# Six of eight accumulators held in PSUM, two copied out by ScalarE, and angle tables built without GpSimd

## The chip, the core and the metric

The kernel runs on one core of a Trainium2 chip, as one program in one launch. The metric is the device time of an execution in microseconds. A core has five engines with one in-order queue of instructions each: TensorE (PE in the profile; its weight loads are PEld), VectorE (DVE), ScalarE (ACT), GpSimd (POOL) and SyncE (SP, which only starts transfers here). Matrix products go into PSUM, which has eight banks of 128 x 512 float32; the rest of the data is in SBUF.

## The reference

A two-layer streaming encoder on T = 576 tokens (a prompt of 512 and a sample of 64), width 1024. A layer is

- one input projection `h = x @ w_in`, split among three mixers: a diagonal state-space model (SSM), banded attention and a retention; each mixer's output is projected, multiplied by a sigmoid gate, and the three are summed, projected by `w_o` and normalised;
- PEER: 8 heads choose 16 experts each out of 128 x 128, and each chosen expert contributes

```
u = u_tab[expert]; act = gelu(u . x); out += gate * act * v_tab[expert]
```

- a gated per-layer input and a last normalisation.

The SSM state is `h_t = a h_(t-1) + b u_t` with complex `a`. The kernel runs it as a real scan after turning the input by `exp(-i theta t)` and turns the result back, so that it needs cos(theta t) and sin(theta t) for 8 blocks of 128 states a layer: two tables of 128 x 576 a block.

## The kernel before

All activations lie feature by token: `XH`, `XL` are eight blocks of 128 features x 576 tokens, the high and the low part of x in the format of the fast float32 product. A product is three matmuls (high x high, high x low, low x high). Weights come by SP into three buffers `wr` (512 KB a block); `split` (L203) makes `wh` with a ScalarE cast (L204) and `wl` with a subtraction (L205), four buffers each.

**Order.** The instructions of each engine are put in order by a planner when the program is made: it takes the program's order as priority and issues what is ready in its own simulated time. On the chip an engine then waits at its next instruction, whatever is behind it. In the first part of a layer, streams of steps (SSM, retention, projections, filling) are woven by `weave` (L137) on a rough clock for TensorE and VectorE.

**Tables.** `rotation` (L419) makes one block's two tables on GpSimd from `rot` (16 angles) and `rot16` (36 multiples of 16 angles): six instructions of 128 x 576. `rot16` is itself made by VectorE at the start, by doubling (L373 to L379). Layer 0 calls `rotation` in `begin` (L708), which is in the SSM stream. The tables of layer 1 are made during layer 0 by `next_tables` (L919), a step at every second step of the attention, and stored to DRAM by SP (L922); layer 1 loads them.

**Gates.** `filling` (L801) computes gate projections while the SSM and the retention hold TensorE up: the first GB = 8 of them, then it waits for the retention.

**Experts.** Tokens NG = 160 to 575 are done densely. `hidden(i)` (L1009) is the first product of the 128 experts with first key i: 24 matmuls of 416 columns into a `lin` bank, then gelu on ScalarE into `act`. The second product adds `v[i]` times gate times `act` to eight output blocks R[0..7]. Gates are built by one-hot products (L1210, L1211), copied by ScalarE (`gs`), stored to DRAM (`gd`), and read back as `gblk`. While the one-hots run, `prefetch` (L1017) computes `hidden` for N_EARLY = 34 experts, whose `act` go to DRAM, and for the first LA + GE = 8; by FR0 and FR its 42 x 8 steps are all placed before or among the one-hot products.

**The loop** (L1283) takes GE = 2 experts at a time. It computes `hidden` for the two that are LA = 6 ahead (or loads an early `act`), multiplies `act` by the gate (GpSimd for every fourth expert, VectorE for the others, L1302), splits it into `Wh`, `Wl`, and then for d = 0..7 does six matmuls (L1324). For d < HELD = 2 the sum stays in PSUM over the whole loop (one bank `bgd`, one `lin`); the other six go to one of four `aux` banks and VectorE adds each to R[d] (L1329). That leaves two `lin` banks to `hidden`. The other 160 tokens are done sparsely by VectorE in the same loop (`advance`, L1270): GpSimd gathers rows of u and v by index (L1237), VectorE takes dot products (L1243) and sums (L1255).

Of the kernel before, what the change touches and what calls it, by code (L numbers as in the profile page):

```python
# [46 lines left out]

GE = 2
LA = 6
N_EARLY = 34  # L50

GB = 8
GS = 7

UR = 0.7
# [10 lines left out]
LS = 0.5  # L66
LE = 0

GG = 4

HELD = 2

VR = 8
LEAD = 3
# [81 lines left out]
def body(ctx, tc, nc, A, O, depth=DEPTH, dbg=None):  # L156
# [153 lines left out]
    cre = cst.tile([128, nst], F32, name="cre")  # L310
    cim = cst.tile([128, nst], F32, name="cim")
    rot = [cst.tile([128, nst, 16], F32, name=f"rot{i}") for i in range(2)]
    rot16 = [cst.tile([128, nst, 36], F32, name=f"rq{i}") for i in range(2)]
    with ExitStack() as c0:
        p0 = pool(c0, "p0")
        t_ = lambda n: p0.tile([128, nst], F32, name=n)
# [53 lines left out]

        for m in (1, 2, 4, 8):
            double(V, rot[0], rot[1], 0, m)
        for i in range(2):  # L373
            V.memset(rot16[i][:, :, 0:1], 1.0 - i)
            V.tensor_copy(rot16[i][:, :, 1:2], rot[i][:, :, 15:16])
        for m in (1, 2, 4, 8, 16):
            double(V, rot16[0], rot16[1], 1, m)
        for i in range(2):
            V.tensor_copy(rot16[i][:, :, 32:36], rot16[i][:, :, 0:4])  # L379

    tables = dr.tile([8, 2, 128, T], F32, name="tables")
    for L in range(depth):
# [6 lines left out]
def run(steps, n=None):  # L389
    for _ in steps if n is None else zip(range(n), steps):  # L390
        pass
# [7 lines left out]
def mixers(tc, env):  # L399
# [6 lines left out]
    with ExitStack() as c:  # L406
# [1 line left out]
        rp = pool(ret, "rp")  # L408
        gt = pool(ret, "gt")
        M = []  # L410
        o36 = lambda t: t.rearrange("p (a b) -> p a b", b=16)

        def col(blk):
            clock[0] += 48 * HF / 2400
# [1 line left out]

        gates = {}

        def rotation(qq, pl, bufs):  # L419

            new = lambda n, b=1: pl.tile([128, T], F32, name=n, bufs=b)
            ct, sn, tx = new("ct", bufs), new("sn", bufs), new("tx")
            c1 = [e.rot16[i][:, qq, :, None].to_broadcast([128, 36, 16]) for i in range(2)]
            c2 = [e.rot[i][:, qq, None, :].to_broadcast([128, 36, 16]) for i in range(2)]
            G.tensor_mul(o36(ct), c1[0], c2[0])
            G.tensor_mul(o36(tx), c1[1], c2[1])
            G.tensor_sub(ct, ct, tx)
            tx = new("tx")
            G.tensor_mul(o36(sn), c1[0], c2[1])
            G.tensor_mul(o36(tx), c1[1], c2[0])  # L430
            G.tensor_add(sn, sn, tx)
            return ct, sn

        def col_steps(blk, out):
# [254 lines left out]
        def ssm():  # L689
# [18 lines left out]
            def begin(q):  # L708
                if L:
                    ct, st = wk("ct", 2), wk("sn", 2)  # L710
                    SY.dma_start(ct, e.tables[q, 0])
                    SY.dma_start(st, e.tables[q, 1])
                else:
                    ct, st = rotation(q, sp, 2)
                if q % 2 == 0:
                    yield from project(q)
                inputs[q] = ct, st, bus.pop(q)
# [111 lines left out]
        with ExitStack() as ca:  # L829
# [88 lines left out]

            def next_tables():  # L919
                for q in range(8):  # L920
                    for i, t in enumerate(rotation(L * 8 + 8 + q, pa, 1)):
                        SY.dma_start(e.tables[q, i], t)  # L922
                    yield

# [69 lines left out]
def peer_ple(tc, env):  # L994
# [8 lines left out]
    with ExitStack() as c:  # L1003
# [5 lines left out]
        def hidden(i):  # L1009
            w = weights(A["uT"][L, i], eng=by[0])  # L1010
            p = lin()
            yield from e.mm3_steps(p, w, XH, XL, (NG, T))
            act = ap_.tile([128, ND_T], F32, name="act", bufs=LA + GE)
            S.activation(act, p[:, :ND_T], AF.Gelu_apprx_tanh)
            acts[i] = act
# [265 lines left out]
        av = A["v"].rearrange("(a p) d -> a p d", p=128)  # L1281

        for e1 in range(0, 128 + LA, GE):  # L1283
            for i in range(e1, min(e1 + GE, 128)):
                if i in acts:
                    continue
                if i in early:
                    acts[i] = ap_.tile([128, ND_T], F32, name="act", bufs=LA + GE)
                    SY.dma_start(acts[i], ad[i])
                else:  # L1290
                    run(hidden(i))
            e0 = e1 - LA
            if e0 < 0:
                continue
            wv = []
            for i in range(e0, e0 + GE):
                act = acts.pop(i)
                if i % IB == 0:
                    gblk = lp.tile([128, NTG, IB, TG], F32, name="gblk", bufs=2)
                    SY.dma_start(gblk, gd[:, :, i:i + IB].rearrange("g j i t -> j g i t"))  # L1300
                a3 = act.rearrange("p (g t) -> p g t", t=TG)
                (G if GG and i % GG == 0 else V).tensor_mul(a3, a3, gblk[:, :, i % IB])  # L1302
                wh = lp.tile([128, ND_T], F32R, name="Wh", bufs=2 * GE)

                wl = (lp.tile([128, ND_T], F32R, name="Wl", bufs=2 * GE) if i > e0 else
                      vraw().bitcast(F32R)[:, :ND_T])
                split(wh, wl, act)
                wv.append(weights(av[L * 128 + i]) + (wh, wl))
# [4 lines left out]
                SY.dma_start(gb3[:, 0], A["ln3_g"][L])  # L1313
                SY.dma_start(gb3[:, 1], A["ln3_b"][L])
            if e0 == 0:
                held = [e.bgd(), lin()][:HELD]
            for a, b in ((NG, HF), (HF, T)) if fin else ((NG, T),):
                for d in range(ND):
                    hold = d < HELD
                    p = held[d][:, a - NG:b - NG] if hold else bank()[:, :b - a]  # L1320
                    w = slice(d * 128, (d + 1) * 128)
# [4 lines left out]
                                      stop=(j == GE - 1 and g == 2 and (fin or not hold)), skip_group_check=hold)  # L1326
                    if hold and not fin:
                        continue
                    V.tensor_add(R[d][:, a:b], R[d][:, a:b], p)  # L1329
            done = advance(done, (e0 + GE) / PACE)  # L1330
        m32 = load(lp, A["c_m32"], [128, NG2], "m32")
# [132 lines left out]
```

## Time and profile before

| | |
|---|---|
| median of 3 executions | 4293.08 us (4280.81 to 4308.05) |
| the profiled execution | 4261.82 us, span 4260.0 us |
| mean granted TensorE clock | 0.974 of full speed |
| busy: PE, PEld | 4050.0 us (95%), 3789.8 us (89%) |
| busy: DVE, ACT, POOL | 3433.5 us (81%), 1562.5 us (37%), 1435.8 us (34%) |

Times inside a profile count from the span's start. A row of the windows view is one stretch with the busy time and the number of instructions of each engine, the granted clock, and the share of time in which the 16 DMA engines were busy. A row of the waits view says which engine and line waited for which, for how long in total, how often, and the longest. In a timeline or a group of lines, `out<-in` are the program's names.

### The profile page before, as it was taken

The numbers are of one execution on the slowest core, as the hardware profiler recorded it, in microseconds if no ns is written. First come the engines' busy times: TensorE is split into PE (matmuls) and PEld (weight loads), VectorE is DVE, ScalarE is ACT, GpSimd is POOL, SyncE is SP. The second block draws the span as 40 slices with busy tenths as digits, with TensorE's granted clock in tenths as the row PEclk, the third lists the DMA queues.
The fourth block names the chain that finished last, engine by engine and source line by source line (L and its number), as shares of the span: only waits on it lengthen the run. The fifth ranks groups of instructions, "written<-read, shape, count | busy, mean of one in ns | idle before, by whom it ended". The sixth has DMA issues, their size and how long they took to land.

```text
span 4260.0 us, 65840 instructions
## 1 busy us (share of the span) xinstructions
PE 4050.0 (95%) x25032; PEld 3789.8 (89%) x25032; DVE 3433.5 (81%) x6827; ACT 1562.5 (37%) x2600; POOL 1435.8 (34%) x1050
## 2 busy tenths in 40 slices
PE   6998999898999999999999999999989999999998
PEld 6787899798999999999787889897989999999997
DVE  8944459987999989999678344698979999999985
ACT  3223433376333333333432243333843333233324
POOL 4634123301545445443100011332035444454421
PEclk8999999999999999999999999999999999999999
DMA  3123222277998989898232222124789999889961
GB/s 114 56 76 113 67 72 79 96 262 266 321 336 315 330 297 331 302 336 283 68 99 83 83 85 78 60 81 137 282 287 331 322 327 317 311 310 321 320 210 43
DMA packets 353886, 873.78 MB, mean 205 GB/s; under 512 B 33184, under 2 KB 169504, under 8 KB 350240
## 3 DMA queue, kind: packets, MB, share of 16 engines
q1 hardware_dynamic: 261408, 533.98, 36.4%
q0 software_dynamic: 92160, 335.59, 22.1%
q8 instruction: 196, 3.21, 0.3%
q14 instruction: 122, 1.00, 0.1%
HBM read 788.09 MB, written 79.00 MB: 204 GB/s over the span
## 4 chain that ended last, share of the span: by engine, by line
PE 71%; DVE 15%; DMA 7%; POOL 3%; issue 2%; ACT 1%; SPq 0%; POOLq 0%; DVEq 0%; ACTq 0%
PE lin L221 38%; PE aux L1324 16%; DMA wr<-in_uT 3%; PE lin L1324 3%; PE bgd L1324 3%; PE aux L221 2%; PE aux L132 2%; DVE wl L205 1%; DVE s L1052 1%; DVE t L132 1%; PE aux L265 1%; PE aux L1210 1%; PE aux L1211 1%; DMA gr<-in_u,gidx 1%; DVE hi L132 1%
## 5 line engine op out<-in xcount | busy, mean ns | idle before, releaser
L221 PE MATMUL lin<-XH,wh 128*128 128x288 f32 (+1 forms) x4288 | 1411.9, 330 | 25.1 <-ACT wh L204 13.7
L221 PE MATMUL lin<-XH,wl 128*128 128x288 f32 (+1 forms) x4288 | 1392.8, 325 | 9.5 <-DVE wl L205 9.5
L221 PE MATMUL lin<-XL,wh 128*128 128x288 f32 (+1 forms) x4288 | 1396.3, 326 | 0.0
L204 ACT CAST wh<-wr 128x1024 fp32r<-128x1024 f32 x692 | 713.0, 1047 | 1861.8 <-PE aux L1324 675.6
L205 DVE TENSOR_TENSOR wl<-wr,wh 128x1024 fp32r<-128x1024 f32 x628 | 784.0, 1264 | 379.8 <-ACT wh L204 309.1
L221 PEld LDWEIGHTS lin<-XH,wh 128*128 128x128 f32 x4288 | 815.3, 190 | 65.2 <-issue 29.2
L221 PEld LDWEIGHTS lin<-XH,wl 128*128 128x128 f32 x4288 | 814.4, 190 | 18.3 <-DVE wl L205 10.5
L221 PEld LDWEIGHTS lin<-XL,wh 128*128 128x128 f32 x4288 | 815.7, 190 | 12.1 <-issue 7.3
L1324 PE MATMUL aux<-Wh,wh 128*128 128x416 f32 (+1 forms) x1560 | 552.0, 354 | 36.1 <-DVE R L1329 36.1
L1324 PE MATMUL aux<-Wh,wl 128*128 128x416 f32 (+1 forms) x1560 | 550.0, 353 | 0.0
L1237 POOL DMA_INDIRECT gr<-in_v,gidx x320 | 426.7, 1333 | 364.7 <-DVE gr L1243 215.4
L1237 POOL DMA_INDIRECT gr<-in_u,gidx x320 | 414.5, 1295 | 374.2 <-DVE acc L1255 214.5
L1329 DVE TENSOR_TENSOR R<-R,aux 128x416 f32<-128x416 f32 x780 | 426.0, 571 | 18.5 <-PE aux L1324 17.1
L1255 DVE SCALAR_TENSOR_TENSOR acc<-gr,wg,acc 128x1024 f32<-128x1024 f32 x316 | 407.6, 1290 | 12.1 <-DMA gr<-in_v,gidx 12.0
L1243 DVE SCALAR_TENSOR_TENSOR gr<-gr,xtok 128x1024 f32<-128x1024 f32 x320 | 406.1, 1272 | 10.0 <-DMA gr<-in_u,gidx 9.9
L1324 PEld LDWEIGHTS aux<-Wh,wh 128*128 128x128 f32 x1560 | 295.7, 190 | 45.8 <-DVE R L1329 45.2
L1302 POOL TENSOR_TENSOR act<-act,gblk 128x416 f32<-128x416 f32 x64 | 96.4, 1507 | 636.5 <-DMA gblk<-gd 453.2
L1324 PEld LDWEIGHTS aux<-Wh,wl 128*128 128x128 f32 x1560 | 295.8, 190 | 3.7
L1324 PE MATMUL aux<-gr,wh 128*128 128x416 f32 x780 | 272.8, 350 | 0.0
L1324 PE MATMUL aux<-Wl,wh 128*128 128x416 f32 x780 | 272.1, 349 | 0.0
L205 POOL TENSOR_TENSOR wl<-wr,wh 128x1024 fp32r<-128x1024 f32 x64 | 155.5, 2430 | 323.0 <-ACT wh L204 272.6
L1212 ACT ACTIVATE gs<-aux 128x512 f32<-128x512 f32 x208 | 206.7, 1166 | 0.0
(405 smaller groups left out, 5937.2 us busy)
## 6 DMA issues: line engine op xcount, KB each, us to landing
wr<-in_uT SPq DMA_DIRECT2D x256, 512.0 KB
wr<-in_v SPq DMA_DIRECT2D x256, 512.0 KB
gd<-gs SPq DMA_DIRECT2D x26, 2048.0 KB
gblk<-gd SPq DMA_DIRECT2D x64, 832.0 KB
wr<-in_w_in SPq DMA_DIRECT2D x92, 512.0 KB
wr<-in_peer_wq SPq DMA_DIRECT2D x32, 512.0 KB
ad<-act SPq DMA_DIRECT2D x68, 208.0 KB
act<-ad SPq DMA_DIRECT2D x68, 208.0 KB
```

What stands on the lines that cost most here:

```text
L132: return f(out, *a, **k)
L204: S.copy(hi, src)
L205: (eng or V).tensor_sub(lo, src, hi)
L221: PE.matmul(out[:, :b - a], wt[:, s], x[:, a:b], start=(first and k == 0 and g == 0), stop=(last and k == n - 1 and g == 2))
L265: PE.matmul(var[:1, :HF], ones1, sq, start=(d == 0), stop=(d == ND - 1))
L1212: S.activation(gs[:, :, o + t:o + t + 4].rearrange("p i t -> p t i"), p.rearrange("p (t i) -> p t i", t=4), AF.Copy, scale=1.0 / GSCALE)
L1237: G.indirect_dma_start(out=r, out_offset=None, in_=A[table], in_offset=bass.IndirectOffsetOnAxis(ap=gidx[:, s:s + 1], axis=0))
L1243: V.scalar_tensor_tensor(r, r, 1.0, xtok[s // 128], op0=OP.mult, op1=OP.mult, accum_out=dots[:, s:s + 1])
L1255: V.scalar_tensor_tensor(o, r, w, o, op0=OP.mult, op1=OP.add)
L1302: (G if GG and i % GG == 0 else V).tensor_mul(a3, a3, gblk[:, :, i % IB])
L1324: PE.matmul(p, x[:, w], y[:, a - NG:b - NG], start=(j == 0 and g == 0 and (e0 == 0 or not hold)), stop=(j == GE - 1 and g == 2 and (fin or ...
L1329: V.tensor_add(R[d][:, a:b], R[d][:, a:b], p)
```

## The change

Four edits: (1) HELD is 6, so that blocks 0 to 5 stay in PSUM (bgd, two lin, three aux banks); blocks 6 and 7 are copied from the one remaining aux bank to SBUF by ScalarE and added to R by VectorE from there. The order of the blocks is 0, 1, 2, 6, 3, 4, 5, 7; of the two `hidden` (or loads) of a pass, one stands before the products and the rest between block 6 and block 3. (2) All gate products of the loop are on VectorE. (3) `rotation` starts from the 16 angles and doubles: per doubling two ScalarE multiplications by a column and two VectorE instructions; `rot16` is gone. (4) N_EARLY is 38, GB is 10.

```diff
-N_EARLY = 34
-GB = 8
+N_EARLY = 38
+GB = 10
-GG = 4
-HELD = 2
+HELD = 6
+ORDER = (0, 1, 2, 6, 3, 4, 5, 7)
...
-        for i in range(2):
-            V.memset(rot16[i][:, :, 0:1], 1.0 - i)
-            V.tensor_copy(rot16[i][:, :, 1:2], rot[i][:, :, 15:16])
-        for m in (1, 2, 4, 8, 16):
-            double(V, rot16[0], rot16[1], 1, m)
-        for i in range(2):
-            V.tensor_copy(rot16[i][:, :, 32:36], rot16[i][:, :, 0:4])
...
-        def rotation(qq, pl, bufs):
-
-            new = lambda n, b=1: pl.tile([128, T], F32, name=n, bufs=b)
-            ct, sn, tx = new("ct", bufs), new("sn", bufs), new("tx")
...
-            G.tensor_mul(o36(ct), c1[0], c2[0])
-            G.tensor_mul(o36(tx), c1[1], c2[1])
-            G.tensor_sub(ct, ct, tx)
-            tx = new("tx")
-            G.tensor_mul(o36(sn), c1[0], c2[1])
-            G.tensor_mul(o36(tx), c1[1], c2[0])
-            G.tensor_add(sn, sn, tx)
+        def rotation(V, qq, pl, bufs):
+
+            ct, sn = (pl.tile([128, T], F32, name=n, bufs=bufs) for n in ("ct", "sn"))
+            tx = pl.tile([128, 2, 256], F32, name="tx")
+            c0, s0 = (r[:, qq] for r in e.rot)
+            S.copy(ct[:, :16], c0)
+            S.copy(sn[:, :16], s0)
+            m = 16
+            while m < TP:
+                c, s = (c0, s0) if m == 16 else (ct[:, :m], sn[:, :m])
+                cm, sm = c[:, m - 1:m], s[:, m - 1:m]
+                S.activation(tx[:, 0, :m], s, AF.Copy, scale=sm)
+                S.activation(tx[:, 1, :m], c, AF.Copy, scale=sm)
+                V.scalar_tensor_tensor(ct[:, m:2 * m], c, cm, tx[:, 0, :m], op0=OP.mult, op1=OP.subtract)
+                V.scalar_tensor_tensor(sn[:, m:2 * m], s, cm, tx[:, 1, :m], op0=OP.mult, op1=OP.add)
+                m *= 2
+            for t in (ct, sn):
+                S.copy(t[:, TP:], t[:, :T - TP])
             return ct, sn
...
         for e1 in range(0, 128 + LA, GE):
-            for i in range(e1, min(e1 + GE, 128)):
-                if i in acts:
-                    continue
-                if i in early:
-                    acts[i] = ap_.tile([128, ND_T], F32, name="act", bufs=LA + GE)
-                    SY.dma_start(acts[i], ad[i])
-                else:
-                    run(hidden(i))
+            ahead = iter([i for i in range(e1, min(e1 + GE, 128)) if i not in acts])
+
+            def first_products(n):
+                for _, i in zip(range(n), ahead):
+                    if i in early:
+                        acts[i] = ap_.tile([128, ND_T], F32, name="act", bufs=LA + GE)
+                        SY.dma_start(acts[i], ad[i])
+                    else:
+                        run(hidden(i))
+
             e0 = e1 - LA
             if e0 < 0:
+                first_products(GE)
                 continue
+            first_products(1)
...
-                (G if GG and i % GG == 0 else V).tensor_mul(a3, a3, gblk[:, :, i % IB])
+                V.tensor_mul(a3, a3, gblk[:, :, i % IB])
...
-                held = [e.bgd(), lin()][:HELD]
+                held = [e.bgd(), lin(), lin(), bank(), bank(), bank()]
             for a, b in ((NG, HF), (HF, T)) if fin else ((NG, T),):
-                for d in range(ND):
+                for d in ORDER:
+                    if d == 3:
+                        first_products(GE)
                     hold = d < HELD
...
                     if hold and not fin:
                         continue
+                    if not hold:
+                        t = lp.tile([128, ND_T], F32, name="vo", bufs=2)[:, :b - a]
+                        S.copy(t, p)
+                        p = t
                     V.tensor_add(R[d][:, a:b], R[d][:, a:b], p)
```

## Rows read from the trace of the kernel before

**Rows 1.** Windows: both expert loops from first to last product, and a stretch without stall.
```profile
1042.42:2044.00 1001.58, 984.05 (x5187) 969.00 (x5188) 945.57 (x1319) 311.02 (x436) 470.19 (x351) 0.99 0.89 312
3136.90:4137.00 1000.10, 981.25 (x5186) 967.31 (x5187) 945.90 (x1319) 311.06 (x436) 463.85 (x351) 0.99 0.89 312
1391.00:1498.00 107.00, 107.00 (x568) 105.91 (x567) 105.23 (x145) 33.45 (x47) 48.72 (x39) 1.00 0.93 326
```

**Rows 2.** Waits over the whole span: total us, times, longest.
```profile
PE aux L1324 <- DVE R L1329: 36.1, 24, 5.2
...
ACT wh L204 <- DMA wr<-in_v: 125.8, 38, 10.9
...
ACT wh L204 <- DMA wr<-in_uT: 93.1, 18, 9.8
```

**Rows 3.** Timeline: VectorE and ScalarE at one of the longest stalls.
```profile
1565.69 1.23 DVE L205 TENSOR_TENSOR wl<-wr,wh 128x1024 fp32r<-128x1024 f32 x1 [5.66 <-ACT wh L204]
...
1564.61 1.04 ACT L204 CAST wh<-wr 128x1024 fp32r<-128x1024 f32 x1 [9.74 <-DMA wr<-in_uT]
```

**Rows 4.** Waits, then timeline of ScalarE, SP and GpSimd: entry to the first loop.
```profile
PE bgd L1324 <- ACT Wh L204: 33.8, 2, 17.0
...
1024.60 3.64 ACT L1212 ACTIVATE gs<-aux 128x512 f32<-128x512 f32 x4
...
1034.70 1.23 SPq L1300 DMA_DIRECT2D gblk<-gd  x2
...
1040.39 1.41 POOL L1302 TENSOR_TENSOR act<-act,gblk 128x416 f32<-128x416 f32 x1 [195.41 <-DMA gblk<-gd]
```

**Rows 5.** Windows: same stretches of SSM and early attention, layer 0 and 1 in turn.
```profile
34.26:105.22 70.96, 53.01 (x326) 47.80 (x325) 65.54 (x80) 17.81 (x41) 50.03 (x25) 0.81 0.26 80
2185.02:2229.33 44.31, 43.00 (x293) 40.22 (x292) 35.16 (x53) 16.57 (x39) 0.00 (x0) 0.92 0.41 122
105.22:205.64 100.42, 94.46 (x574) 74.10 (x573) 89.91 (x120) 25.41 (x51) 70.62 (x23) 0.95 0.18 58
2229.33:2318.51 89.18, 88.16 (x573) 70.60 (x572) 74.86 (x120) 25.67 (x51) 0.00 (x0) 1.00 0.29 90
205.64:280.65 75.01, 65.97 (x393) 51.20 (x393) 44.20 (x95) 15.04 (x29) 4.71 (x2) 0.95 0.14 45
...
280.65:351.13 70.48, 54.83 (x399) 53.93 (x398) 16.80 (x11) 15.63 (x28) 65.35 (x51) 0.91 0.36 127
2393.55:2446.38 52.83, 52.83 (x400) 52.65 (x398) 11.83 (x11) 15.84 (x28) 2.03 (x4) 1.00 0.33 108
```

**Rows 6.** Timeline, layer 0: VectorE with and without GpSimd's table work beside it.
```profile
88.35 0.74 DVE L132 TENSOR_TENSOR t<-ct,t 128x576 f32<-128x576 f32 x1
89.02 1.71 DVE L132 TENSOR_TENSOR hr<-hr,t 128x576 f32<-128x576 f32 x1
...
88.50 1.61 POOL L429 TENSOR_TENSOR sn<-rq,rot 128x576 f32<-128x576 f32 x1 [0.69 <-DVE hi L132]
```

**Rows 7.** SP's own waits at table stores; timeline of ScalarE behind them.
```profile
SPq L922 <- POOL sn L431: 25.8, 7, 4.3
...
336.74 1.04 ACT L204 CAST wh<-wr 128x1024 fp32r<-128x1024 f32 x1 [10.76 <-DMA wr<-in_w_in]
```

**Rows 8.** Groups of instructions: the loop's additions and its gelu.
```profile
L1329 DVE TENSOR_TENSOR R<-R,aux 128x416 f32<-128x416 f32 x780 | 426.0, 571 | 18.5 <-PE aux L1324 17.1 <-issue 0.5
...
L1014 ACT ACTIVATE act<-lin 128x416 f32<-128x416 f32 x256 | 134.0, 524 | 0.0
```

**Rows 9.** Timeline: small operations of ScalarE and VectorE.
```profile
18.68 0.22 ACT L335 ACTIVATE sth<-th 128x16 f32<-128x16 f32 x1 [0.80 <-DVE th L334]
...
362.77 0.51 ACT L884 ACTIVATE st<-st,mxt 128x256 f32<-128x256 f32 x1 [2.27 <-DVE mxt L883]
...
29.42 0.17 DVE L364 TENSOR_TENSOR s__206<-rq 128x16 f32<-128x16 f32 x1
...
40.55 0.42 DVE L364 TENSOR_TENSOR s__206<-rq 128x256 f32<-128x256 f32 x1
```

More of the change, by code (lines that the diff above doesn't have):

```diff
@@ L312, in body @@
     rot = [cst.tile([128, nst, 16], F32, name=f"rot{i}") for i in range(2)]
-    rot16 = [cst.tile([128, nst, 36], F32, name=f"rq{i}") for i in range(2)]
     with ExitStack() as c0:
@@ L410, in mixers @@
         M = []
-        o36 = lambda t: t.rearrange("p (a b) -> p a b", b=16)
         def col(blk):
@@ L417, in mixers @@
         gates = {}
-        def rotation(qq, pl, bufs):
-            new = lambda n, b=1: pl.tile([128, T], F32, name=n, bufs=b)
-            ct, sn, tx = new("ct", bufs), new("sn", bufs), new("tx")
-            c1 = [e.rot16[i][:, qq, :, None].to_broadcast([128, 36, 16]) for i in range(2)]
-            c2 = [e.rot[i][:, qq, None, :].to_broadcast([128, 36, 16]) for i in range(2)]
-            G.tensor_mul(o36(ct), c1[0], c2[0])
-            G.tensor_mul(o36(tx), c1[1], c2[1])
-            G.tensor_sub(ct, ct, tx)
-            tx = new("tx")
-            G.tensor_mul(o36(sn), c1[0], c2[1])
-            G.tensor_mul(o36(tx), c1[1], c2[0])
-            G.tensor_add(sn, sn, tx)
+        def rotation(V, qq, pl, bufs):
[15 more added lines that the diff above has]
+                S.copy(t[:, TP:], t[:, :T - TP])
             return ct, sn
@@ L713, in begin @@
                 else:
-                    ct, st = rotation(q, sp, 2)
+                    ct, st = rotation(V, q, sp, 2)
                 if q % 2 == 0:
@@ L920, in next_tables @@
                 for q in range(8):
-                    for i, t in enumerate(rotation(L * 8 + 8 + q, pa, 1)):
+                    for i, t in enumerate(rotation(V, L * 8 + 8 + q, pa, 1)):
                         SY.dma_start(e.tables[q, i], t)
```

## The prediction

> **What bounds the kernel now.** I read the busy shares of the whole page first, then windows over one stage at a time, since a share over the span hides which engine ends a stage last. In the two expert loops TensorE and VectorE both look full [rows 1]. The stretch without a stall settles who leads: 568 matmuls in 107.0 us is 0.188 us a matmul, and at that pace the first loop's 5187 take 977 us of its 1001.6, the second's 5186 take 977 of 1000.1. TensorE is therefore the bound, and 24 + 23 = 48 us of both loops are lost to stalls and to a clock below full (0.99). VectorE, at 945.6 us, is nearly as full and cannot catch up once it is late.
>
> The waits name the loss: TensorE waited 36.1 us in 24 places for VectorE's addition to R, which has to free an aux bank [rows 2]. The place of a long one shows what was behind it. ScalarE stood 9.74 us at a cast whose weight block had not landed; VectorE stood 5.66 us at the subtraction that needs this cast, with the additions behind it in its queue [rows 3]. So a late weight is the root, VectorE's queue the path, and the four aux banks the cushion that ran out.
>
> Before each loop stands one more hole: TensorE waits 33.8 us in two places for the first `Wh` [rows 4]. The last gates leave PSUM by ScalarE from 1024.60, go to DRAM and come back from 1034.70, and the gate product starts at 1040.39; no other product is left to run.
>
> Last, I set layer 0 beside layer 1, where the same instructions run with tables loaded [rows 5]. Layer 0 takes 71.0 us against 44.3, 100.4 against 89.2, and 70.5 against 52.8: 26.7 + 11.2 + 17.7 us more. GpSimd is busy with tables in all three (50.0, 70.6 and 65.4 us), against 0, 0 and 2.0. In the first two VectorE is the sufferer: an instruction of 128 x 576 takes 0.74 us alone and 1.71 beside a table product [rows 6]. In the third it is SP: it waited 25.8 us for `sn` tables at their stores [rows 7], weight loads stand behind those stores, and ScalarE waited 10.76 us for a weight.
>
> **The change, part by part.**
>
> *Held blocks.* Each pass adds two blocks to R in place of six. Per loop 63 x 4 x 0.571 us [rows 8] = 144 us leave VectorE. 32 gate products come to it from GpSimd, at the addition's 0.571 us as the nearest row 18 us, so it falls from 946 to about 820 us of a loop. ScalarE gains two copies a pass, 128 x 0.524 (gelu of the same shape, from PSUM as well) = 67 us on its 311 [rows 1, 8]. None of this is on the path as long as the copies are prompt. Behind a copy stand the casts in ScalarE's queue, and before the next product of an aux bank TensorE has at least 18 matmuls (three blocks), 3.4 us; with a `hidden` among them 7.9 us. For `lin`, now one bank, four blocks lie between two `hidden`: 24 matmuls, 4.5 us. A late VectorE no longer stops TensorE, except at a weight. What may be worth up to 48 us [rows 1] and, if the late weights stop TensorE all the same, nothing, I take at 30: the additions' 36.1 us [rows 2], less some that come back at weights, and a little of the clock. What is late next is the weight load itself: 218.9 us of ScalarE's waiting [rows 2] at 0.89 to 0.93 of the DMA engines' time [rows 1]. SP's order changes too: the second `uT` load, or `act` load, of a pass moves behind the two loads of `v`.
>
> The row shows that four aux banks did not prevent these waits, since 36.1 us arose with them. The Trainium skill (Perfetto Trace Analysis, Matmuls) says that independent matmul groups should rotate through several PSUM banks, so that the copying out of one lies beside the products of the next; the change leaves one bank to rotate. By that rule the loop's term would be a loss; the first rival prices it.
>
> *N_EARLY.* The prefetch is 368 steps and the stage places 336, so four `hidden` (96 matmuls, 18.1 us) are left for the hole of 17 us before each loop, and each loop is 18.1 us shorter. The early ones add four stores and four loads of `act` a layer on SP, but save loading four weights in the loop. The hole's chain grows by the time that four weight blocks, 2.1 MB, take from the gates' transfers: none if they landed before, 6.7 us at the loop's 312 GB/s [rows 1]. Without that the hole is full (17 + 18.1 becomes 18.1), with it 23.7 us long: a gain per layer of 17 to 11.4 us; I take 15, 30 in all.
>
> *Tables.* A table is 14 ScalarE and 10 VectorE instructions of 16 to 256 columns: 14 x 0.22 to 14 x 0.51 = 3.1 to 7.1 us and 10 x 0.17 to 10 x 0.42 = 1.7 to 4.2 us [rows 9]. Eight blocks in layer 0's SSM put 14 to 34 us on VectorE. Against it the doubling of `rot16` goes (30 instructions, 5 to 13 us by the same rows), and so does GpSimd's drag. The whole excess of the first two stretches is 37.9 us, the upper bound; the lower is 38 - 34 = 4. I take 24, nearer to the upper, since most doublings are shorter than 256. The two engines take turns: five doublings of two ScalarE instructions and the VectorE one that waits for them, at the middle of these rows 5 x (2 x 0.37 + 0.30) = 5.2 us, and four copies, 1.5 us, make a table's chain about 7 us. In the SSM it is covered except for the first block, since each table is asked for a block ahead.
>
> The other eight run in the attention of layer 0, where ScalarE and VectorE use 15.6 and 16.8 of 70.5 us. If the 16 stores hold SP as before, nothing comes back; if not, all 17.7 us. ScalarE and VectorE are idle there, but a table's chain of about 7 us is not much shorter than now, so I take 12.
>
> *GB.* Two more gates may fill SSM time. In the third stretch TensorE spends 75.0 us on 393 matmuls, while 400 take 52.8 us where nothing holds it [rows 5]: over 20 us a layer are unfilled. A gate is 48 matmuls, 6.3 us; two in each layer are worth 0 to 25 us. I take 12, half.
>
> **Sum:** 30 + 30 + 24 + 12 + 12 = 108 us. The profiled execution, 4261.8 us, would become 4154; it lies 31 us below the median of 4293.1, which I lower by the same 108: 4185 us.
>
> **Rivals.**
>
> *One bank waits for ScalarE* (slower). If ScalarE's waits for weights, 125.8 + 93.1 = 218.9 us [rows 2], all pass to TensorE through the single aux and lin banks, the loops lose 219 in place of 48, 171 more; with the other 78 us gained, 4386 us. It decides from 126 us, 58% of those waits. For it: the queue is strictly in order. Against it: 56 waits average 3.9 us, about the cushion of 3.4 to 7.9, and VectorE's slack frees `wr` buffers earlier. Chance 0.08.
>
> *The loops don't gain*, since the transfers set the stalls: 78 us, 4215. For it rows 3. Against it the new cushion is no shorter. Chance 0.2.
>
> *The tables give nothing*: chains hold SP and VectorE as GpSimd did. 108 - 36 = 72 us, 4221. For it the chain's length; against it rows 6. Chance 0.14.
>
> *The four blocks miss the hole*, because they run before the last one-hots or their weights delay the gates' way: 78 us, 4215. Chance 0.08.
>
> The forecast has 0.5.
>
> **From these to the numbers.** With all bounds at their best (48 + 34 + 38 + 18 + 25 = 163 us) the time is 4130; two of the middle rivals together give about 42 us, 4251. The range 4125 to 4262 leaves out the first rival and the worst pairs. About 1%, 43 us, is what a measurement tells from no change: faster by more 0.83, within 0.10 (pairs of rivals), slower 0.07 (nearly all the first rival).
>
> **What would show it.** Right: PE waits for R gone, and TensorE's matmuls in the loops at 0.188 us; loops near 970 us; no wait for `Wh` over 5 us before the loops; the first two stretches of layer 0 within 15 us of layer 1's; no SP wait at table stores above a microsecond. Wrong: TensorE waiting for ScalarE's copy or gelu in a loop; ScalarE's waits for weights grown; a hole of over 20 us at the loops' entry.

## The result: 4144.3 us, 3.5% faster

The changed kernel takes 4144.32 us (median of 4 runs, 4131.98 to 4146.18), the kernel before 4293.99 beside it; the ratio is 0.9645, 95% interval 0.9609 to 0.9681. The forecast was 4185 us in a range of 4125 to 4262. The profiled execution took 4143.22 us (span 4141.4), 1.1 from the median; that of before, 4261.82, was 32 us under its own.

Windows over both expert loops (span; then busy time of PE, PEld, DVE, ACT and POOL; granted clock, DMA share, GB/s) answer [rows 1]:

```profile
1005.74:1972.50 966.76, 959.01 (x5092) 945.47 (x5092) 820.19 (x1095) 363.19 (x559) 427.53 (x313) 1.00 0.90 319
3054.30:4018.50 964.20, 956.98 (x5091) 943.85 (x5091) 820.59 (x1095) 363.30 (x559) 423.97 (x313) 1.00 0.90 320
```

The loops are 34.8 and 35.9 us shorter. Four experts' first products, 96 matmuls or 18.1 us, left each; the remaining 16.7 and 17.8 are stalls that are gone. VectorE fell from 946 to 820 us, as foretold; ScalarE rose to 363 (378 by the prediction's terms).

Waits of the whole span, then TensorE's own in the first loop alone, answer [rows 2]:

```profile
ACT vo L1332 <- PE aux L1325: 352.5, 125, 6.1
...
DVE act L1301 <- DMA act<-ad: 113.2, 35, 7.1
...
DVE R L1334 <- ACT vo L1332: 53.6, 66, 1.6
...
ACT wh L203 <- DMA wr<-in_v: 50.7, 19, 4.8
```

```profile
PE bgd L1325 <- DVE wl L204: 7.0, 8, 1.8
PE bgd L1325 <- issue: 0.5, 1, 0.5
```

TensorE no longer waits for R. The copy waits for TensorE, not the other way round. ScalarE's 125.8 us of waiting for `v` weights became 50.7, and its 93.1 for `uT` left the list. What is left for TensorE are short stops at a held block for the low part of a weight.

The timeline of ScalarE and SP at the entry of the first loop answers [rows 4]:

```profile
986.55 3.93 ACT L1207 ACTIVATE gs<-aux 128x512 f32<-128x512 f32 x4
...
1005.15 1.04 ACT L203 CAST Wh<-act 128x416 fp32r<-128x416 f32 x2 [0.64 <-DVE act L1301]
...
990.50 0.33 SPq L1210 DMA_DIRECT2D gd<-gs  x1
...
998.50 0.38 SPq L1299 DMA_DIRECT2D gblk<-gd  x1
```

The gates' way through DRAM is no shorter than before, 8.0 us from the store to the first load against 6.4 (1028.27 to 1034.70), but TensorE works through it: 96 matmuls of `hidden` lie between the last one-hot product (987.34) and the loop's first (1005.74). The hole of 17.0 and 17.2 us became a full stretch of 18.4 and 18.8.

Windows over the SSM and early attention (first, second and fourth stretch of layer 0; first and fourth of layer 1) answer [rows 5]:

```profile
34.04:90.38 56.34, 54.86 (x351) 48.62 (x350) 45.64 (x91) 31.69 (x92) 0.00 (x0) 0.90 0.33 104
90.38:196.12 105.74, 100.62 (x645) 82.34 (x644) 90.20 (x165) 42.51 (x114) 0.00 (x0) 0.97 0.20 64
...
271.10:312.06 40.96, 40.21 (x303) 39.93 (x302) 20.86 (x49) 26.93 (x80) 1.37 (x5) 1.00 0.50 172
2111.16:2156.52 45.36, 44.33 (x293) 41.39 (x292) 35.25 (x53) 16.46 (x39) 0.00 (x0) 0.89 0.39 120
2325.49:2365.60 40.11, 40.11 (x303) 39.93 (x302) 9.37 (x9) 12.31 (x22) 2.50 (x4) 1.00 0.36 116
```

Layer 0 lost its excess over layer 1 almost wholly: 56.3 against 45.4 and 41.0 against 40.1. The first two stretches hold 25 and 71 matmuls more than before, which are the two further gates: 96 matmuls of 288 columns, 12.7 us at the 0.132 us a matmul of layer 1's fourth stretch before (400 in 52.8 us). The second stretch is longer for that; the fourth is shorter by the same matmuls.

SP's own waits where the tables are stored answer [rows 7]; the first row is of the kernel before, beside the `sn` row shown there, the others of the changed kernel:

```profile
SPq L922 <- POOL ct L427: 24.8, 7, 4.3
```

```profile
SPq L917 <- DVE ct L422: 21.3, 6, 5.8
...
SPq L208 <- DVE sn L423: 8.9, 3, 3.7
```

SP stood 50.6 us at 14 table stores (25.8 for `sn`, 24.8 for `ct`) and now 21.3 us at 6, all for a `ct`, up to 5.8 us at one. The last row is not a store: L208 loads a weight.

### The profile page after: what moved, and what is told of

Its sections match the earlier page's. It is cut to its first block, busy times and chain, and to the rows that moved or that the text cites. A ratio compares the mean times of both kernels' runs of the same rounds, so it can differ in the third digit from the quotient of the medians.

```text
span 4141.4 us, 65803 instructions
## 1 busy us (share of the span) xinstructions
PE 4025.1 (97%) x25032; PEld 3770.5 (91%) x25032; DVE 3182.1 (77%) x6511; ACT 1732.4 (42%) x3084; POOL 1189.8 (29%) x890
## 4 chain that ended last, share of the span: by engine, by line
PE 79%; DVE 13%; DMA 3%; issue 2%; ACT 1%; POOL 1%; SPq 0%; DVEq 0%; POOLq 0%; ACTq 0%
PE lin L220 42%; PE aux L1325 16%; PE lin L1325 6%; PE bgd L1325 3%; PE aux L220 2%; PE aux L131 2%; DMA act<-ad 2%; DVE wl L204 1%; DVE s L1047 1%; PE aux L1205 1%; PE aux L264 1%; PE aux L1206 1%; DVE t L131 1%; DVE IX L1049 1%; DVE IX L1045 1%
## 5 line engine op out<-in xcount | busy, mean ns | idle before, releaser
L1232 POOL DMA_INDIRECT gr<-in_u,gidx x320 | 446.2, 1394 | 854.6 <-DVE gr L1238 388.1
L1325 PE MATMUL aux<-Wh,wl 128*128 128x416 f32 (+1 forms) x1300 | 454.0, 349 | 0.0
L1325 PE MATMUL aux<-Wh,wh 128*128 128x416 f32 (+1 forms) x1300 | 453.6, 350 | 0.0
L1238 DVE SCALAR_TENSOR_TENSOR gr<-gr,xtok 128x1024 f32<-128x1024 f32 x320 | 388.7, 1217 | 3.3 <-DMA gr<-in_u,gidx 3.3
L1332 ACT COPY vo<-aux 128x416 f32<-128x416 f32 x260 | 129.0, 496 | 362.2 <-PE aux L1325 352.5
L1325 PEld LDWEIGHTS aux<-Wh,wl 128*128 128x128 f32 x1300 | 244.3, 188 | 2.8
L1325 PEld LDWEIGHTS aux<-Wh,wh 128*128 128x128 f32 x1300 | 244.3, 188 | 1.1
L1301 DVE TENSOR_TENSOR act<-act,gblk 128x416 f32<-128x416 f32 x256 | 146.9, 584 | 113.6 <-DMA act<-ad 113.2
L1325 PE MATMUL aux<-gr,wh 128*128 128x416 f32 (+2 forms) x650 | 226.2, 348 | 0.0
L1325 PE MATMUL aux<-Wl,wh 128*128 128x416 f32 (+2 forms) x650 | 225.9, 347 | 0.0
```

The source lines that it names most:

```text
L1232: G.indirect_dma_start(out=r, out_offset=None, in_=A[table], in_offset=bass.IndirectOffsetOnAxis(ap=gidx[:, s:s + 1], axis=0))
L1238: V.scalar_tensor_tensor(r, r, 1.0, xtok[s // 128], op0=OP.mult, op1=OP.mult, accum_out=dots[:, s:s + 1])
L1301: V.tensor_mul(a3, a3, gblk[:, :, i % IB])
L1325: PE.matmul(p, x[:, w], y[:, a - NG:b - NG], start=(j == 0 and g == 0 and (e0 == 0 or not hold)), stop=(j == GE - 1 and g == 2 and (fin or ...
L1332: S.copy(t, p)
```

## The experiments

Each kernel was timed against the kernel before on the same chip. Between the chips the median of before moved from 4276 to 4294 us, so a difference between an experiment and the changed kernel's 4144.3 us is sure to some 18 us only; where it matters, the loops of the two traces are compared. A loop's time below is from the start of its first product to the start of its last. "Lost" is what both loops took over their matmuls at the 0.1884 us of the stretch without a stall [rows 1].

**The kernel before again.** No edit.

> The kernel before, unchanged, with a second profile. The change moved the median by 150 us and the profiled executions by only 118.6 us (4260.0 to 4141.4 us span), because the first profile of before lies 31 us below its own median. Theory A: executions of before differ in how late weight blocks land in the expert loops, so the loops of this profile are longer than 1001.6 and 1000.1 us by up to 15 us each where its span is nearer to 4290, and the rest of the span agrees within 3 us. Theory B: the difference lies outside the loops or is spread evenly over all stages (a slower clock): the loops then make up no more than their half of it. If this profile again takes 4262 us, the profiled executions are shorter for a reason that neither names.

4285.5 us, ratio 1.0014 [1.0000, 1.0029], span 4279.6, 19.6 us over the first profile. The loops (1005.1 and 1001.3) are only 5.4 us longer, so theory A falls and theory B holds in that the difference lies outside them: 13.7 us lie in layer 1 between the start of its SSM and its attention. The next windows show layer 1's stretch behind a hole of 6.26 us (from the start of one matmul to that of the next; TensorE is idle for 5.96 of it), in this order: the kernel before, first profile; the same, second profile; the changed kernel, where that hole is gone; the changed kernel with GB back at 8, an experiment told below:

```profile
2322.00:2370.00 48.00, 39.48 (x210) 26.34 (x209) 25.99 (x62) 9.26 (x19) 4.64 (x2) 0.93 0.10 31
```

```profile
2330.00:2389.00 59.00, 50.54 (x205) 31.24 (x204) 25.64 (x61) 9.27 (x19) 4.57 (x2) 0.74 0.08 25
```

```profile
2252.00:2301.00 49.00, 47.34 (x274) 34.07 (x272) 27.21 (x62) 10.42 (x21) 3.62 (x2) 1.00 0.16 52
```

```profile
2250.00:2308.00 58.00, 50.67 (x209) 31.68 (x207) 26.04 (x61) 8.62 (x18) 3.29 (x2) 0.74 0.09 25
```

The same 205 to 210 matmuls take 11 us more at a granted clock of 0.74 than at 0.93; VectorE's and ScalarE's busy time is the same. From the hole's start to the end of the output products is 45.8 us in the first profile and 57.5 in the second, and there is nothing between: over the eight profiles here with GB at 8, both layers, the stretch took 45.8 to 46.4 us five times and 55.2 to 57.5 eleven times. In layer 1 the first profile is the only short one. In the changed kernel layer 1's hole is gone, more matmuls fit in, and the clock is 1.00; layer 0's hole, 5.96 us idle, is still there.

**Held blocks alone**, with their order, the copies and the place of the first products:

```
-HELD = 2
+HELD = 6
+ORDER = (0, 1, 2, 6, 3, 4, 5, 7)
...
+                    if not hold:
+                        S.copy(t, p)
```

> The kernel before with only the six held blocks, the order of blocks, the split of the two first products and the copies by ScalarE. Theory: the loops lose VectorE's additions as a stop for TensorE. Each loop from 1001 to about 984 us (the 34 us that the two loops of the changed kernel gained beyond the four moved blocks), time lower by 35 to 55 us, ratio 0.987 to 0.992. Rival (gate products): the loops gain only once GpSimd's gate products are gone; then this run is within 10 us of before and the loops stay near 1000. Rival (one bank): TensorE waits for ScalarE's copies; then it is slower than before.

4311.04 us, ratio 1.0065 [1.0043, 1.0086]: slower. The theory fell, and both rivals as they were worded: TensorE never waited for a copy, but 49.3 us in 39 places for a weight's low part. (What the first rival gives as its reason, the gate products, comes back below.) The loops took 1011.2 and 1012.5 us, 17.4 us more than in the second profile of before; of the other 12 us between these two profiles, 9 are the long form of the stretch behind the hole, in layer 0.

**N_EARLY alone.**

```
-N_EARLY = 34
+N_EARLY = 38
```

> The kernel before with only N_EARLY 38. Theory: four first products a layer, 18.1 us, fill the hole of 17 us before each loop and leave the loop; hole plus loop gets 15 to 17 us shorter in each layer, time lower by 30 to 34 us, ratio 0.992 to 0.993. Rival (they miss the hole or hold up the gates): the wait for the first Wh stays over 10 us and the time falls by under 12 us.

4232.47 us, ratio 0.9891 [0.9866, 0.9917]: more than expected. The holes became 18.9 and 19.2 us, full; the loops, 972.4 and 976.1, lost 31.3 us in place of 53.1, so stalls went beyond the matmuls moved out.

**Tables alone** (`rotation` by doubling, `rot16` gone).

> The kernel before with only the tables by doubling on ScalarE and VectorE. Theory: layer 0 of the SSM and the early attention loses GpSimd's drag and the late weight loads behind table stores. The stretch of layer 0 from the SSM's first product to the transposes of the first values, 316.9 us before, becomes 277 to 285 us, time lower by 32 to 40 us, ratio 0.9905 to 0.9925, layer 1 unchanged. Rival (chains hold SP and VectorE as GpSimd did): under 15 us.

4246.4 us, ratio 0.9924 [0.9896, 0.9952], inside the expected range. Layer 0 from its SSM to its attention took 286.6 us against 317.0, a little more than the 277 to 285 expected; the loops (1005.2, 1001.7) did not move.

These three add up to 50 to 60 us of a drop of 150, with one of them slower. Left were GB, and a part that the prediction had counted as a cost alone: the gate products of every fourth expert, which left GpSimd for VectorE.

**GB back at 8 in the changed kernel.**

```
-GB = 10
+GB = 8
```

> The changed kernel with GB back at 8, nothing else undone. Theory C (the two more gates of GB fill TensorE's 6.3 us hole in front of the SSM's output products, and that hole is also what lets the granted clock fall in the 60 us behind it: 0.74 in layer 1 in three of the runs so far, 0.93 in the first profile, 1.00 in the changed kernel): both layers get a hole of some 6 us back and in at least one of them the stretch behind it runs at 0.74 to 0.93, so layer 1 from its first input split to attention goes from 254.6 back to 261 to 275 us and the whole is 12 to 40 us longer than the changed kernel, 4156 to 4185 us, ratio to before 0.968 to 0.977. Rival (GB is worth only the hole, the clock is chance): the holes come back at 12 us for both layers, with the clock as it was, 4156 us, ratio 0.968. Rival (GB hides nothing): no change, 4144 us, ratio 0.9645.

4168.11 us, ratio 0.974 [0.9718, 0.9762]. Layer 1's hole is back, 6.25 us, and the clock behind it falls to 0.74 (fourth row above). From layer 1's first normalised block to attention's first transposition it takes 296.4 us against 277.5; layer 0's transposition comes 7.6 us later. Theory C holds: of layer 1's 18.9 us, 6.3 are the hole and some 11.5 the clock (57.4 us behind the hole's start against 45.8).

**The changed kernel with GpSimd's gate products.**

```
-                V.tensor_mul(a3, a3, gblk[:, :, i % IB])
+                (G if GG and i % GG == 0 else V).tensor_mul(a3, a3, gblk[:, :, i % IB])
```

> The changed kernel with every fourth gate product of the expert loop back on GpSimd (1.65 us each there, 0.58 on VectorE), nothing else undone. Theory P (with six blocks held, a product that sits in GpSimd's queue holds back the gathers behind it; VectorE's accumulations wait for those, and VectorE's split of the pair's second weight block, queued behind them, comes late to TensorE): the stops in front of the held blocks' last product come back as in the held-only kernel, 32 of them and 58 us over both loops instead of 13 and 17, the loops take 980 to 990 us instead of 966 and 964, the whole 4175 to 4190 us, ratio to before 0.973 to 0.978. Rival Q (the stops of the held-only kernel come from the transfers of the weights, whichever engine gates): within 8 us of the changed kernel, ratio 0.963 to 0.967.

4225.76 us, ratio 0.9867 [0.9844, 0.989]: over half of the whole gain is gone, more than theory P had expected. The loops took 1003.8 and 1006.2 us. TensorE's waits of both loops:

```profile
PE bgd L1327 <- DVE wl L206: 58.2, 40, 5.0
```

**Held blocks with the gate products on VectorE**, on the kernel before.

```
-GG = 4
+GG = 0
```

(and the held blocks as above)

> The kernel before with the six held blocks, the new order and the copies as in the held-only kernel, and the gate products all on VectorE. Theory P: the 28 us by which held-only was slower than before turn into a gain, for the stops fall to some 17 us over both loops: loops of 985 to 990 us against 1011.5 and 1012.8 in held-only and 1001 to 1005 before, the whole 4245 to 4265 us, ratio to before 0.991 to 0.996. Rival Q (GpSimd has no part): as held-only, ratio 1.004 to 1.009.

4244.53 us, ratio 0.9912 [0.989, 0.9934]. The loops took 982.8 and 983.6 us; held-only's loss turned into a gain, as theory P had it, with loops a little shorter than its 985 to 990.

**The gate products alone** on VectorE, on the kernel before.

> The kernel before with all gate products of the expert loop on VectorE, and nothing else. Theory P, with two blocks held: VectorE is busy 945 of 1001 us in the loop and takes 32 more products of 0.58 us, 18.7 us a loop, while its adds are what TensorE waits for at the six banks; the gathers come sooner. The first outweighs: loops 1005 to 1020 us, ratio to before 1.000 to 1.008. Rival (the moved products are a gain by themselves, and the held blocks are worth little): loops 985 to 995 us, ratio 0.990 to 0.996.

4237.76 us, ratio 0.9887 [0.9859, 0.9915]. My expectation missed, and the rival with it, for the gain is larger than either had. The loops:

```profile
1058.58:2031.98 973.40, 973.40 (x5184) 963.96 (x5184) 948.82 (x1349) 313.36 (x436) 398.50 (x313) 1.00 0.91 317
3137.50:4112.23 974.73, 973.54 (x5184) 963.77 (x5184) 948.47 (x1349) 313.10 (x436) 405.95 (x313) 1.00 0.91 317
```

TensorE is busy almost without a break, with VectorE at 97% and only two blocks held. The loops are 58.3 us shorter; between the profiles the whole is only 42 us shorter, since the two stretches before the loops grew by 5 us and layer 0's stretch behind its hole took the long form, 9 us more.

So the stalls of [rows 2] went with this edit, though no row read so far had named GpSimd as what TensorE waits for. What carried them is not shown. Rows of the kernel before that bear on it, at the stall of [rows 3]: GpSimd, then SP, then windows of 6 and 21 us:

```profile
1537.28 1.09 POOL L1302 TENSOR_TENSOR act<-act,gblk 128x416 f32<-128x416 f32 x1 [8.59 <-issue]
...
1545.90 0.33 SPq L209 DMA_DIRECT2D wr<-in_uT  x1
```

```profile
1535.00:1541.00 6.00, 6.00 (x33) 5.97 (x33) 6.00 (x10) 2.59 (x4) 3.27 (x3) 1.00 0.25 92
1544.00:1565.00 21.00, 20.04 (x106) 19.46 (x105) 14.70 (x21) 4.20 (x7) 8.16 (x8) 1.00 1.02 379
```

GpSimd stood 8.6 us at a product and then issued ten gathers in 18 us (1538.52 to 1556.17). The DMA engines were busy a quarter of the time (0.25) and then all of it (1.02). The `uT` load that SP had issued last, at 1545.90, lay 18.7 us back when ScalarE's cast could start at 1564.61. That is one place, and a reading. Over the first loop ScalarE waited 99.9 us for expert weights before and 24.7 with this edit. A rival stands untested: the planner put the instructions in a new order. Apart from the gate products, VectorE runs the same 1232 instructions here as before, but only 1002 of them stand in a common order.

**A short GpSimd product in the changed kernel**, to tell its wait from its work: it takes 32 of 416 columns.

```
+                g0 = 1 if i % GG == 0 else 0
+                if g0:
+                    G.tensor_mul(a3[:, :g0], a3[:, :g0], gb[:, :g0])
+                V.tensor_mul(a3[:, g0:], a3[:, g0:], gb[:, g0:])
```

> The changed kernel in which GpSimd takes 32 of the 416 columns of every fourth gate product, and VectorE the other 384. GpSimd's instruction is short, but it waits for the same gate block and the same activation as the whole product did in the kernel with the products back on GpSimd (4225.8 us). Theory P, as a wait: its sequencer stood 5.5 us (median) at each product with the gathers behind it, and that alone is the price: loops of 1000 to 1006 us, 4205 to 4226 us, ratio to before 0.981 to 0.988. Rival (the price is what GpSimd does while it multiplies, 1.1 to 3.6 us a product beside VectorE's work): loops within 8 us of the changed kernel's 966 and 964, the whole 4144 to 4160 us, ratio 0.965 to 0.971.

4222.06 us, ratio 0.9859 [0.9831, 0.9888]; loops of 1000.1 and 999.7 us, as theory P had it. 69.5 of the 79.6 us that GpSimd's products cost in the loops remain, though GpSimd multiplies a thirteenth and its instruction takes half as long: it is mostly the wait. Here the planner is no rival: apart from the gate products, 978 of VectorE's 980 instructions of the first loop, and all of ScalarE's and SP's, stand in the changed kernel's order (965 of VectorE's with the whole products). The gate line's instructions (least, median and greatest duration in ns) in four kernels: before, held-only, the changed kernel with GpSimd's products, and with the short ones. The EVENT_SEMAPHORE rows are GpSimd's sequencer standing at the product:

```profile
L1302 POOLq EVENT_SEMAPHORE  x66: 17/590/157081, 841.9 to 4066.2; - x66
L1302 POOL TENSOR_TENSOR act<-act,gblk x64: 1082/1316/3104, 1040.4 to 4075.7; 128x416 f32<-128x416 f32 x64
```

```profile
L1307 POOLq EVENT_SEMAPHORE  x66: 17/5470/156966, 855.7 to 4112.9; - x66
```

```profile
L1303 POOLq EVENT_SEMAPHORE  x66: 17/3729/81802, 1002.2 to 4030.5; - x66
```

```profile
L1306 POOLq EVENT_SEMAPHORE  x68: 17/3858/82309, 1004.1 to 4023.8; - x68
L1306 POOL TENSOR_TENSOR act<-act,gblk x64: 252/818/2792, 1004.3 to 4036.5; 128x32 f32<-128x32 f32 x64
```

The median wait was 3.7 to 5.5 us with six blocks held. Before it was 0.6, but 22 of its 66 waits were above 5 us as well. How one looks in the changed kernel with GpSimd's products (GpSimd, then SP):

```profile
1141.59 1.33 POOL L1234 DMA_INDIRECT gr<-in_u,gidx  x1 [0.30 <-issue]
1154.42 1.09 POOL L1303 TENSOR_TENSOR act<-act,gblk 128x416 f32<-128x416 f32 x1 [11.51 <-issue]
1155.67 1.80 POOL L1234 DMA_INDIRECT gr<-in_v,gidx  x1
...
1146.15 0.36 SPq L1287 DMA_DIRECT2D act<-ad  x1
```

GpSimd stands 11.5 us at a product, while an early `act` that SP issued at 1146.15 is on its way, and issues no gather meanwhile. Who pays is in VectorE's waits for gathered rows in the first loop: in the changed kernel, with GpSimd's products, and with the short ones.

```profile
DVE acc L1250 <- DMA gr<-in_v,gidx: 5.6, 7, 2.2
DVE gr L1238 <- DMA gr<-in_u,gidx: 2.3, 2, 1.3
```

```profile
DVE gr L1240 <- DMA gr<-in_u,gidx: 26.2, 18, 4.7
DVE acc L1252 <- DMA gr<-in_v,gidx: 24.5, 17, 4.4
```

```profile
DVE gr L1240 <- DMA gr<-in_u,gidx: 30.2, 15, 8.2
DVE acc L1252 <- DMA gr<-in_v,gidx: 21.2, 23, 2.8
```

7.9 us became 50.7 and 51.4, in loops that are 37 and 34 us longer. While GpSimd stands, gathers come late; VectorE stands at them, with the weight splits behind it in its queue; and TensorE waits for the splits (12.0 us in both loops of the changed kernel, 58.2 with GpSimd's products). These waits of TensorE are 46 of the 79.6 us; in 29 more it counts as busy with the same matmuls, at a mean clock of 0.99 against 1.00. The kernel before differs: its VectorE waited only 12.1 us for gathers in the first loop, so this path is shown with six blocks held and not for the stalls of [rows 2].

**Two blocks held, all else changed.** Since the gate products alone had loops of 973 us and the held blocks with them 983, this looked like a better kernel.

```
-HELD = 6
-ORDER = (0, 1, 2, 6, 3, 4, 5, 7)
+HELD = 2
```

> The changed kernel with the expert loop's blocks as before (two held, six added from PSUM by VectorE in their old order, no copies on ScalarE) and all else of the change: gate products on VectorE, N_EARLY 38, GB 10, the doubled tables. Theory P says now that the moved gate products are the loops' whole gain and the held blocks cost some: with the gate products alone moved the loops took 973.4 and 974.7 us, with six blocks held as well 982.8 and 983.6. With four first products fewer (18.1 us) the loops come to 955 to 958 us against 966.4 and 963.9 in the changed kernel, the whole to 4120 to 4132 us, ratio to before 0.961 to 0.965, faster than the changed kernel by 10 to 20 us. Rival (VectorE, then busy some 940 of 955 us, is the bound, and only the held blocks let the other parts of the change show): loops of 966 to 980 us, 4145 to 4175 us, ratio 0.967 to 0.975.

4372.32 us, ratio 1.02 [1.0164, 1.0236]. Both theories missed by over 190 us. The loops took 1082.0 and 1076.8 us. Its first loop as a window, then, by line, the chain that ended last between 1100 and 1900 us:

```profile
1003.45:2085.42 1081.97, 1004.86 (x5088) 961.45 (x5088) 942.65 (x1347) 314.32 (x430) 420.03 (x313) 0.97 0.84 285
```

```profile
by line: DMA wr<-in_uT 17.5%; DVE acc L1252 13.7%; DMA wr<-in_v 13.4%; DVE gr L1240 10.0%; DVE wl L205 9.3%; issue 8.5%; DVE R L1326 6.7%; PE aux L1321 6.0%; ACT wh L204 3.6%; PE lin L221 2.4%; PE lin L1321 2.0%; ACT Wh L204 1.7%; DVE Wl L2
```

No engine is full (VectorE 87%, DMA 0.84): the chain goes round from a weight's load through its cast and split, behind VectorE's other work, back to the buffer that the next load needs. In the kernel with the gate products alone every piece of the same chain was TensorE's. The programs of the two loops differ by N_EARLY alone, but the planner's order does too: 848 of VectorE's 1232 instructions stand in a common order. With the shorter loop VectorE's 943 us would have to fit into some 955, 98.7%. Whether the loop tips there, or by the new order, is open.

**Natural order and both first products ahead of the blocks**, in the changed kernel.

```
-ORDER = (0, 1, 2, 6, 3, 4, 5, 7)
+ORDER = (0, 1, 2, 3, 4, 5, 6, 7)
...
-            first_products(1)
+            first_products(GE)
```

> The changed kernel with the blocks in their natural order, so that the two which are not held follow each other on the one bank that is left, and with both first products of a pass ahead of its blocks. If that bank has to be empty before TensorE goes on, it waits once a pass for the whole of ScalarE's copy, 0.5 us and the way there and back, and longer where a cast is ahead of it in ScalarE's queue: 0.7 to 2 us in 128 half-passes (64 a layer), loops of 1010 to 1090 us less what the order itself costs, the whole 4230 to 4400 us, ratio 0.988 to 1.027. Rival (the order is worth little, since ScalarE is prompt and only 37% busy): within 25 us of the changed kernel, ratio 0.965 to 0.970.

4211.69 us, ratio 0.9838 [0.9806, 0.9869], between the two expectations. TensorE's waits in the first loop:

```profile
PE bgd L1325 <- DVE wl L204: 18.9, 23, 5.4
PE aux L1325 <- ACT vo L1332: 2.3, 3, 1.2
```

The order matters, 67 us of the whole and 59 in the loops, but mostly not by the bank: the two neighbours on it cost 2.3 us of waits in this loop, while the stops at held blocks for a weight's low part grew from 7.0 to 18.9. Which of the two edits does that was not separated.

**VectorE adds straight from the bank**, in the changed kernel.

```
-                    if not hold:
-                        t = lp.tile([128, ND_T], F32, name="vo", bufs=2)[:, :b - a]
-                        S.copy(t, p)
-                        p = t
```

> The changed kernel without ScalarE's copies: VectorE adds the two blocks that are not held straight from their bank, in the changed order. If the one bank needs a prompt engine, TensorE waits wherever VectorE, at over 80% and strictly in order, has an accumulation and a split or two ahead of the addition (1.2 to 5 us against the 3.4 us of three blocks): waits of TensorE for R appear again, 20 to 80 us over both loops, the whole 4160 to 4225 us, ratio 0.971 to 0.987. Rival (VectorE has the slack, and the copies only load ScalarE): no such waits, within 10 us of the changed kernel or faster, ratio 0.962 to 0.967.

4179.9 us, ratio 0.9757 [0.9729, 0.9785], as expected. TensorE's waits for R are back in the first loop:

```profile
PE aux L1325 <- DVE R L1330: 19.6, 13, 3.0
```

So the copies on ScalarE are worth 36 us (35 in the loops) where one bank is left, with the order that the planner gave each kernel.

**The loops of eight kernels beside each other** (sum of both, and lost):

| | gate products partly on GpSimd | all on VectorE |
|---|---|---|
| 2 held, N_EARLY 34 | 2006.4, lost 53.1 | 1948.1, lost -5.2 |
| 6 held, N_EARLY 34 | 2023.8, lost 70.4 | 1966.5, lost 13.1 |
| 2 held, N_EARLY 38 | 1948.5, lost 31.3 | 2158.7, lost 241.5 |
| 6 held, N_EARLY 38 | 2009.9, lost 92.7 | 1930.3, lost 13.2 |

(Those with N_EARLY 38, but for 1948.5, have the tables and GB of the change as well, which lie outside the loops.) The first entry is from the second profile of before; the first profile has 2001.1, lost 47.8. No row or column has a price of its own. The gate products are worth 57 to 80 us, or cost 210. The held blocks cost 17 to 18 us at N_EARLY 34, and at 38 cost 61 or gain 228. Together, held blocks and vector gates lose 13 us whatever N_EARLY is; that is what lets N_EARLY's moved matmuls show in full. From kernel to kernel the planner's order changes as well, except along the two rows with six blocks held, where the order of VectorE's 980 instructions in the first loop, the gate products left out, is the same but for 1 and 15. So the 57 and 80 us of those rows are the products' own; the other differences are prices of an edit with its new order.

## Why the prediction was right, step by step

*The sum.* 108 us forecast; 118.6 between the two profiles, 138 against the second profile of before. I had lowered the median by the sum and so assumed that the profile's 31 us below it would stay. They did not: 13.7 of them lay in layer 1, 11.7 of these behind its hole, which the change fills; 5.4 lay in the loops, and both are in the drop of 150 between the medians. The 12 us from 138 to 150 were not traced.

*Held blocks, 30.* The loops' loss fell from 47.8 us (48 in the prediction) to 13.2, so 34.6: the size was right, by luck, for the reason was not. The step said that VectorE's additions, freed, take TensorE's waits with them, and counted the 32 gate products of a loop only as 18 us more for VectorE. The runs show that held blocks by themselves are slower, and that without the moved gate products the changed kernel's loops lose 92.7 us: what was put down as a cost carries the gain. "A late weight is the root" [rows 3] stopped too early. GpSimd's waits at the gate product stood in the trace of before and were not read; that they make the weights late there is not shown.

*N_EARLY, 30.* Right in mechanism and size: 36.2 us of matmuls left the loops, the holes' stretches grew by 1.4 and 1.6 us (18.4 and 18.8 for 17.0 and 17.2), 33 us net. The 6.7 us that the gates' transfers might have lost came to 1.6 (8.0 for 6.4), behind TensorE's matmuls.

*Tables, 24 + 12.* Layer 0's first two stretches went from 171.4 us to 162.1 with 12.7 us of gates added, 22.0 us; the fourth from 70.5 to 41.0, of which 12.7 is the gates moved out, 16.8 us. Of these 38.8 us some 7.6 are GB's, by the kernel with GB back at 8, and tables alone gave 30.4 in the same stretches: 36 was near, a little high. The drag on VectorE was real, but the pair in [rows 6] does not show it: the instruction of 0.74 us ran from 88.35 to 89.09, for the most part beside a GpSimd product too (from 88.50). A group's mean in layer 0's first two stretches does, before and in the changed kernel:

```profile
L132 DVE TENSOR_TENSOR t<-sn,bu 128x576 f32<-128x576 f32 x14 | 15.4, 1104 | 8.6 <-POOL sn L431 8.0 <-ACT bu L704 0.6
```

```profile
L131 DVE TENSOR_TENSOR t<-sn,bu 128x576 f32<-128x576 f32 x14 | 10.5, 751 | 5.5 <-ACT bu L699 5.4
```

That SP would no longer wait above a microsecond at a store was wrong (5.8 us): the stores of a pair of tables follow the last pair's by 8 to 18 us, by some 9 with GpSimd. That ScalarE's weights come in time all the same is what the fourth stretch shows; why was not tried. ScalarE's multiplications of 128 columns by 16 took 0.29 to 0.34 us, inside the 0.22 to 0.51 of [rows 9].

*GB, 12.* Undersized: 24 us between the medians when it is taken back, 21 between the profiles. The prediction had the hole filled; what it missed was the clock behind the hole, some 11 us in layer 1. Layer 0's hole it did not fill.

*The rivals.* One bank did not wait for ScalarE: no such wait in the changed kernel's loops, 4.7 us in both loops of the kernel with neighbours. The Trainium skill (Perfetto Trace Analysis, Matmuls) asks that independent groups rotate through several PSUM banks; here one bank is enough: with a copy of 0.50 us on ScalarE TensorE does not wait with three or more held blocks between two uses, and hardly with the two uses back to back. Without the copies it waits for the one bank 38.3 us in both loops. "The loops don't gain" would have been true of the change without the gate products: 2009.9 us with them on GpSimd.

## What to carry to other kernels

A busy share says nothing of what an in-order engine holds back while it stands: read how long its sequencer stands at each kind of instruction (the long waits, not the median alone), what is queued behind, and who waits for that, also on an engine that is 34% busy. Where queues feed each other, parts of a change have no separate prices: try pairs before you trust a sum, and before you drop a part that looks like a cost. Where a planner orders every kernel anew, compare the engines' order of two kernels before you put their difference down to the edit. And compare the granted clock of a stretch before comparing its time between two kernels.

## What was not expected of the hardware

- The clock behind a short hole has two outcomes: after the 6.26 us hole in layer 1 the stretch ran at 0.93 in one profile of the same kernel and at 0.74 in the next (part of it at 1.2 GHz in place of 2.4), 11.7 us apart. Without the hole it was 1.00, in the changed kernel.
- A GpSimd product of 128 x 32 took 0.82 us (median), one of 128 x 416 1.32 to 1.65, and VectorE 0.58 for the latter.
